# A decoder layer on one core: separate 256-wide matmuls for two of three PSUM banks, all weight sums on VectorE, another place for the first sum and another way to spread a norm row

## The chip, the cores and the metric

The kernel runs on one core of one Trainium2 chip. The metric is the device time of one launch in microseconds (us), median of several runs; each comparison runs both kernels on the same chip. The profile is one execution taken by the hardware profiler, with a time of its own.

## The reference

One decoder layer over 512 tokens of width 2048, all in float32:

```python
u = rms_norm(h, ln_mix_pre)
o_rec = hgrn2_mixer(...)               # 8 heads, gated recurrence
o_att = dilated_attention_mixer(...)   # 8 heads
h = h + rms_norm(concat(o_rec, o_att) @ w_out, ln_mix_post)
# MLP: w_up is 2048 x 11264, w_down 5632 x 2048
up = rms_norm(h, ln_ffn_pre) @ w_up
up = conv_b + sum(pad[:, j:j + S] * conv_w[j] for j in range(3))
gate, val = split(up, 2)
h = h + rms_norm((gelu(gate) * val) @ w_down, ln_ffn_post)
h = h + (p @ w_pe) * sigmoid(h @ w_pg)
```

## The kernel before

Every large product runs in fp32r (a float32 operand cut to fewer bits) with both operands split into a high and a low part: a product is hi·hi + hi·lo + lo·hi. ACT makes the high part by a cast, DVE the low part by a subtraction (`split_pair`, L623 to L628, for w_up; `split_to`, L180/L181, for activations).

**Start (L197 to L245).** The four token tiles xt of x and the row ln_mix_pre are loaded on SP's queue; the row comes four times 256 KB, a partition broadcast straight from HBM (L208). ACT squares xt, DVE scales it by the row and the inverse root (L235), PE turns it (L241) and the splits go to uT. The first weight units raw_hi are loaded in between.

**The up-projection (L619 to L960)** is the longest stage. The 512 tokens are two halves of 256 (a and b below), the 2048 inputs two halves of 1024 (eight k-blocks of 128), and the 11264 columns 44 groups j, each of two 128-column blocks (the gate's and the value's). One group is thus a 2 x 2 by 2 x 2 block product and is done with seven products instead of eight (Strassen in Winograd's form). It needs weight sums: s5 = w12 + w22, then w12 + w11, s5 + w11 (product 6) and w21 + the result (product 3). `operands(j)` makes them: before the change s5 is added on DVE for j = 1 and even j (L875), and for odd j from 3 on by a load on SP's queue and an accumulating load on POOL's queue (L870, L871); the sum of w12 is an accumulating load on POOL's queue for j > 1 (L877). w11 and w21 are summed on DVE (L880, L885). The activations' sums are made once, ahead of the stage, as eight arrays ua (`second_half`, `last_turns`), each holding the high part ah and the low part al of 256 tokens side by side.

`product(o, ops, i, first)` (L644) adds product i into a PSUM bank of 512 columns. Per k-block it issues one joined matmul of the weights' high part with [ah | al], 512 wide (L649), so that hi·al lands in the right half of the bank, and one of the low part with ah, 256 wide (L650), into the left half. Three banks serve a group: psa takes products 1, 6, 7, 4 one after another and is read after each; psb takes product 2 (read once); psc products 5 and 3. `fold` (L895) adds a psb or psc bank, 512 wide, to an SBUF copy of psa (xx, ub or uc; L897), and then the two halves of the sum together (L898). `Group` calls these in the stages begin (products 1 and 2), middle (6, 5, 7), end (4, 3) and `gate` (convolution and GELU). The stages of neighbouring groups interleave.

**Between the output projection and the stage** `second_half` finishes token tiles 2 and 3: residual (L717 to L730, with the reductions L717 and L729), scaling by ln_ffn_pre (`scale`, L735), turns on PE (`turn_half`, L703), and the activations' sums (L754 to L761). At the same time the p-embedding's products run on PE (L826 to L828) and group 0's weights are loaded (`load_group`, L639). `early_products` does products 1 and 2 of group 0 ahead; `early_sums` (L665) makes the first sums (L669 to L671), s5_0 in a tile of its own in the pool `wo`. y[t] is token tile t, 128 x 2048; its first half is `y[t][:, k1]`.

The order of the instructions on each engine is not the order of the code. A scheduler places them by priorities (`tc.high_priority`: PRI_W for weights, PRI_E for reads of PSUM) as soon as their operands and buffers are free by its own reckoning, and an engine then runs its list strictly in order: an instruction that waits holds up all behind it.

Of the kernel before, what the change touches and what calls it, by code (L numbers as in the profile page):

```python
# [10 lines left out]
F32 = mybir.dt.float32  # L11
# [4 lines left out]
ALU = mybir.AluOpType  # L16
PSUM = bass.MemoryType.PSUM

P = 128
S = 512  # L20
D = 2048
# [36 lines left out]
def trunk(ctx, tc, x, p, ln_mix_pre, w_in, lb_logits, hgrn_norm, w_out, ln_mix_post,  # L58
          ln_ffn_pre, w_up, conv_w, conv_b, w_down, ln_ffn_post, w_pe, w_pg,
          c_dist, c_level, out):  # L60
    nc = tc.nc
# [134 lines left out]

    with tc.tile_pool(name="pre", bufs=2) as pre:  # L197
        ln_b = pre.tile([P, D], F32, bufs=1, name="ln_b")
        xts = []
        for t in range(TT):  # L200
            xt = pre.tile([P, D], F32, tag="xt", bufs=4, name=f"xt{t}")
            for c in range(0, D, D if t else S):
                w = D if t else S
                nc.sync.dma_start(xt[:, c : c + w], x[0, t * P : (t + 1) * P, c : c + w])
            xts.append(xt)
            if t == 0:
                for c in range(0, D, S):
                    nc.sync.dma_start(ln_b[:, c : c + S], ln_mix_pre[0:1, c : c + S].partition_broadcast(P))  # L208
            if t < 2:
                load_unit(w_in[0], t * S, C_I, 4, S, f"hi0_{t}")  # L210
        for t in range(TT):
            xs = pre.tile([P, D], F32, tag="xs", name=f"xs{t}")
            ss = pre.tile([P, 1], F32, tag="ss", name=f"ss{t}")
            rs = pre.tile([P, 1], F32, tag="rs", name=f"rs{t}")
            if t == 0:
                s4 = pre.tile([P, 4], F32, bufs=1, name="s4")
                for g in range(4):
                    gg = slice(g * S, (g + 1) * S)
                    nc.scalar.activation(xs[:, gg], xts[t][:, gg], AF.Square, accum_out=s4[:, g : g + 1])
                nc.vector.tensor_reduce(ss, s4, axis=mybir.AxisListType.X, op=ALU.add)  # L220
            else:
                nc.scalar.activation(xs, xts[t], AF.Square, accum_out=ss)
            ahead = 1 if t else 0
            xl = [None] * 4
            for g in range(ahead):
                gg = slice(g * S, (g + 1) * S)
                xl[g] = pre.tile([P, S], F32, tag="xl", bufs=6, name=f"xl{t}_{g}")
                nc.gpsimd.tensor_tensor(xl[g], xts[t][:, gg], ln_b[:, gg], op=ALU.mult)
            power(rs, ss, 1, D)
            for g in range(4):  # L230
                gg = slice(g * S, (g + 1) * S)
                if g < ahead:
                    nc.vector.tensor_scalar(xs[:, gg], xl[g], rs[:, 0:1], None, op0=ALU.mult)
                else:
                    nc.vector.scalar_tensor_tensor(  # L235
                        xs[:, gg], xts[t][:, gg], rs[:, 0:1], ln_b[:, gg], op0=ALU.mult, op1=ALU.mult
                    )
                ps = aux.tile([P, 4, P], F32, tag="aux", name=f"xtr{t}_{g}")
                for i in range(4):
                    kb = g * 4 + i  # L240
                    nc.tensor.transpose(ps[:, i, :], xs[:, kb * P : (kb + 1) * P], ident)  # L241
                split_to(uT[g][:, :, 0, full[t]], uT[g][:, :, 1, full[t]], ps)


        hrow = pre.tile([2 * HG, P], F32, bufs=1, name="hrow")  # L245
        nc.sync.dma_start(hrow[0:HG, :], lb_logits.rearrange("a (h k) -> (a h) k", k=P))
        nc.sync.dma_start(hrow[HG : 2 * HG, :], hgrn_norm.rearrange("a (h k) -> (a h) k", k=P))
        hps = aux.tile([P, S], F32, tag="aux", name="hps")
        nc.tensor.transpose(hps[:, : 2 * HG], hrow, ident[: 2 * HG, : 2 * HG])
        nc.vector.tensor_copy(norm_c, hps[:, HG : 2 * HG])  # L250
        lg = pre.tile([P, HG], F32, bufs=1, name="lg")
        nc.vector.tensor_copy(lg, hps[:, :HG])
        dl = pre.tile([P, HG], F32, bufs=1, name="dl")
        nc.vector.tensor_tensor(dl, lg, lg, op=ALU.subtract)
        nc.scalar.activation(dl, dl, AF.Exp)
        inv = pre.tile([P, HG], F32, bufs=1, name="inv")
        nc.vector.reciprocal(inv, dl)
        nc.vector.tensor_tensor(dl, dl, inv, op=ALU.mult)
        nc.vector.tensor_tensor(lb_c, dl, dl, op=ALU.subtract)
        nc.vector.tensor_scalar(oml_c, lb_c, -1.0, 1.0, op0=ALU.mult, op1=ALU.add)  # L260
        crow = pre.tile([2 * NFB, 4, P], F32, bufs=1, name="crow")
        for j in range(3):
            nc.sync.dma_start(crow[:, j, :], conv_w[0, j, :].rearrange("(c k) -> c k", k=P))
        nc.sync.dma_start(crow[:, 3, :], conv_b[0, :].rearrange("(c k) -> c k", k=P))
        cps = aux.tile([P, 4, 2 * NFB], F32, tag="aux", name="cps")
        for j in range(4):
            nc.tensor.transpose(cps[:, j, :], crow[:, j, :], ident[: 2 * NFB, : 2 * NFB])
        nc.vector.tensor_copy(conv_c, cps)
# [352 lines left out]
    H8 = KB // 2  # L621
# [8 lines left out]
    def weights(j, k, i):  # L630
        c = i * DFF + j * P
        return w_up[0, k * H8 * P : (k + 1) * H8 * P, c : c + P].rearrange("(k p) n -> p k n", p=P)
# [8 lines left out]
        return raws  # L641


    def product(o, ops, i, first):  # L644
        hi, lo = ops[i]
        for kb in range(H8):
            u = ua[i][kb // 4][:, kb % 4] if i == 4 else ua[i][:, kb]
            both = u.rearrange("p a t -> p (a t)")
            nc.tensor.matmul(o, hi[:, kb, :], both, start=first and kb == 0, stop=False, skip_group_check=True)  # L649
            nc.tensor.matmul(  # L650
                o[:, : 2 * P], lo[:, kb, :], u[:, 0, :], start=False, stop=kb == H8 - 1, skip_group_check=True
            )

    def early_products():
        raws, ops = load_group(0, rawp), {}
# [6 lines left out]
        product(b, ops, 2, True)  # L662
        return raws, ops, a, b

    def early_sums(first, pool):  # L665
        raws, ops = first[:2]
        s5 = pool.tile([P, H8, P], F32, tag="s5e", bufs=1, name="s5_0")
        w11, w12, w22 = raws[0][:, :, 0, :], raws[0][:, :, 1, :], raws[1][:, :, 1, :]
        nc.vector.tensor_tensor(s5, w12, w22, op=ALU.add)  # L669
        nc.vector.tensor_tensor(w12, w11, w12, op=ALU.add)  # L670
        nc.vector.tensor_tensor(w11, s5, w11, op=ALU.add)  # L671
        ops[6] = split_pair(w11, P, "u0_6")
        ops[5] = split_pair(s5, P, "u0_5")
# [5 lines left out]
    with tc.tile_pool(name="wo", bufs=2) as wo:  # L679
# [158 lines left out]
        first = early_products()  # L838
        last_turns(2)
        for _ in late:  # L840
            pass
        early_sums(first, wo)
        last_turns(3)

    homes = {"A": act_slot, "B": lambda tag, name: b_slot(int(tag[1:]), name)}
# [12 lines left out]
    with tc.tile_pool(name="ml", bufs=2) as ml:  # L858
        HT = 2 * P

        def operands(j):
            r1, r2 = first[0] if j == 0 else load_group(j, ml if j % 2 else rawp)
            w11, w12, w21, w22 = r1[:, :, 0, :], r1[:, :, 1, :], r2[:, :, 0, :], r2[:, :, 1, :]
            ops = first[1] if j == 0 else {}
            with tc.high_priority(PRI_W):
                if j:
                    by_dma = (j > 1 and j % 2 == 1, j > 1)
                    s5 = ml.tile([P, H8, P], F32, tag="s5", name=f"s5_{j}")
                    if by_dma[0]:
                        nc.sync.dma_start(s5, weights(j, 0, 1))  # L870
                        nc.gpsimd.dma_start(s5, weights(j, 1, 1), accum_op=ALU.add)  # L871
                    ops[1] = split_pair(w11, P, f"u{j}_1")
                    ops[2] = split_pair(w21, P, f"u{j}_2")
                    if not by_dma[0]:
                        nc.vector.tensor_tensor(s5, w12, w22, op=ALU.add)  # L875
                    if by_dma[1]:
                        nc.gpsimd.dma_start(w12, weights(j, 0, 0), accum_op=ALU.add)  # L877
                    else:
                        nc.vector.tensor_tensor(w12, w11, w12, op=ALU.add)
                    nc.vector.tensor_tensor(w11, s5, w11, op=ALU.add)  # L880
                    ops[6] = split_pair(w11, P, f"u{j}_6")
                    ops[5] = split_pair(s5, P, f"u{j}_5")
                ops[7] = split_pair(w12, P, f"u{j}_7")
                ops[4] = split_pair(w22, P, f"u{j}_4")
                nc.vector.tensor_tensor(w21, w21, w11, op=ALU.add)  # L885
                ops[3] = split_pair(w21, P, f"u{j}_3")
            return ops
# [6 lines left out]

        def fold(dst, src, ps):  # L895
            with tc.high_priority(PRI_E):
                nc.vector.tensor_tensor(src, src, ps, op=ALU.add)  # L897
                nc.vector.tensor_tensor(dst, src[:, :HT], src[:, HT:], op=ALU.add)  # L898

        class Group:  # L900
# [207 lines left out]
```

## Time and profile before

| what | value |
|---|---|
| median of 3 runs | 2534.76 us (2534.52 to 2535.32) |
| profiled execution, its own time | 2539.58 us |
| span of that execution, first to last instruction | 2537.8 us |
| mean granted TensorE clock | 0.993 of full speed |
| instructions | 31312 |
| busy: PE, PEld (weight loads), DVE, ACT, POOL | 98 %, 82 %, 63 %, 44 %, 9 % |
| HBM traffic | 335 MB read, 28 MB written |

A busy share is an average over stages: in the up-projection DVE is far busier than over the whole span. Matmuls are pipelined, so the record of one lasts longer than the distance from its start to the next one's; what a stream of them costs is read from the starts. What stands behind an arrow in brackets is the time an engine was idle ahead of a row and what ended it.

### The profile page before, as it was taken

How to read it: one execution, taken by the hardware profiler on the slowest of the kernel's cores; microseconds unless marked ns; L12 is line 12 of the kernel's file. 1: busy time of each engine (PE TensorE's matmuls, PEld its weight loads, DVE VectorE, ACT ScalarE, POOL GpSimd, SP SyncE). 2: the span in 40 equal slices, each digit the busy share in tenths (PEclk: the TensorE clock that was granted, in tenths of full speed). 3: DMA queues.
4: the chain of work that ended last, by engine and by line, in shares of the span. 5: the costliest groups of instructions: out<-in, count | busy, mean ns of one | idle time of the engine just before them, and what ended most of it. 6: DMA issues, size and time to landing. Idle time of an engine off the chain costs nothing. (4 is left out here: it accounts for less than half of the span.)

```text
span 2537.8 us, 31312 instructions
## 1 busy us (share of the span) xinstructions
PE 2477.9 (98%) x12357; PEld 2087.4 (82%) x12357; DVE 1590.5 (63%) x2199; ACT 1122.9 (44%) x1538; POOL 233.3 (9%) x255
## 2 busy tenths in 40 slices
PE   8999999999999977999999999999999999999999
PEld 6888888888888866888888888888888888887787
DVE  5467377434352567898998988989852233347733
ACT  4454365233342454655555555555542232124421
POOL 1000000000000010111111111111110000002300
PEclk9999999999999998999999999999999999999999
DMA  5222222322234574887877878778654233245642
GB/s 197 89 84 92 91 84 92 112 92 83 92 116 154 201 235 121 182 186 167 179 170 170 183 162 179 173 170 185 158 196 140 100 125 125 99 141 195 210 134 88
DMA packets 397280, 364.86 MB, mean 144 GB/s; under 512 B 9948, under 2 KB 318156, under 8 KB 396492
## 3 DMA queue, kind: packets, MB, share of 16 engines
q1 hardware_dynamic: 316412, 286.82, 36.3%
q0 software_dynamic: 75568, 67.12, 14.2%
q10 hardware_dynamic: 5152, 8.92, 1.0%
q8 instruction: 97, 1.59, 0.2%
q14 instruction: 51, 0.42, 0.1%
HBM read 335.03 MB, written 27.79 MB: 143 GB/s over the span
## 5 line engine op out<-in xcount | busy, mean ns | idle before, releaser
L649 PE MATMUL psa<-ua,hi_u 128*128 128x512 f32 x1408 | 504.1, 399 | 3.6 <-ACT ub L892 1.7
L626 ACT CAST hi_u<-raw_u 128x1024 fp32r<-128x1024 f32 x264 | 277.7, 1052 | 304.2 <-PE psa L649 161.2
L650 PE MATMUL psa<-ua,lo_u 128*128 128x256 f32 x1408 | 395.7, 281 | 1.3 <-DVE lo_u L627 1.3
L627 DVE TENSOR_TENSOR lo_u<-raw_u,hi_u 128x1024 fp32r<-128x1024 f32 x264 | 322.2, 1221 | 43.8 <-ACT hi_u L626 43.3
L649 PEld LDWEIGHTS psa<-ua,hi_u 128*128 128x128 f32 x1408 | 264.5, 188 | 70.2 <-ACT ub L892 2.4
L650 PEld LDWEIGHTS psa<-ua,lo_u 128*128 128x128 f32 x1408 | 266.0, 189 | 2.0 <-DVE lo_u L627 2.0
L649 PE MATMUL psc<-ua,hi_u 128*128 128x512 f32 x704 | 252.7, 399 | 0.0
L135 DVE TENSOR_TENSOR lo_dn<-raw_dn,hi_dn 128x1024 fp32r<-128x1024 f32 x72 | 88.1, 1224 | 230.7 <-ACT hi_dn L134 230.6
L168 PE MATMUL ps_dn<-lo_dn,gT 128*128 128x512 f32 x576 | 224.2, 389 | 0.6 <-DVE lo_dn L135 0.6
L169 PE MATMUL ps_dn<-hi_dn,gT 128*128 128x512 f32 x576 | 224.1, 389 | 0.0
L167 PE MATMUL ps_dn<-hi_dn,gT 128*128 128x512 f32 x576 | 223.9, 389 | 0.0
L650 PE MATMUL psc<-ua,lo_u 128*128 128x256 f32 x704 | 197.7, 281 | 0.0
L134 ACT CAST hi_dn<-raw_dn 128x1024 fp32r<-128x1024 f32 x72 | 75.8, 1054 | 242.6 <-PE ps_dn L169 234.2
L649 PEld LDWEIGHTS psc<-ua,hi_u 128*128 128x128 f32 x704 | 132.3, 188 | 32.9
L650 PEld LDWEIGHTS psc<-ua,lo_u 128*128 128x128 f32 x704 | 133.0, 189 | 0.1
L168 PEld LDWEIGHTS ps_dn<-lo_dn,gT 128*128 128x128 f32 x576 | 108.1, 188 | 23.6 <-DVE lo_dn L135 1.0
L167 PEld LDWEIGHTS ps_dn<-hi_dn,gT 128*128 128x128 f32 x576 | 108.0, 188 | 22.4
L649 PE MATMUL psb<-ua,hi_u 128*128 128x512 f32 x352 | 126.5, 399 | 0.0
L169 PEld LDWEIGHTS ps_dn<-hi_dn,gT 128*128 128x128 f32 x576 | 108.1, 188 | 22.3
L135 DVE TENSOR_TENSOR lo_wo<-raw_wo,hi_wo 128x1024 fp32r<-128x1024 f32 x48 | 58.7, 1224 | 76.3 <-ACT hi_wo L134 76.3
L135 DVE TENSOR_TENSOR lo_pg<-raw_pg,hi_pg 128x1024 fp32r<-128x1024 f32 x40 | 51.6, 1290 | 85.9 <-ACT hi_pg L134 85.9
L167 PE MATMUL ps_pg<-hi_pg,h2T 128*128 128x512 f32 x256 | 100.2, 391 | 3.3 <-ACT h2T L180 3.3
(328 smaller groups left out, 5412.0 us busy)
## 6 DMA issues: line engine op xcount, KB each, us to landing
raw_u<-in_w_up SPq DMA_DIRECT2D x176, 512.0 KB, 5.4
raw_dn<-in_w_down SPq DMA_DIRECT2D x36, 1024.0 KB, 5.0
raw_wo<-in_w_out SPq DMA_DIRECT2D x24, 1024.0 KB, 5.1
raw_u<-in_w_up POOLq DMA_DIRECT2D x42, 512.0 KB, 6.3
raw_pg<-in_w_pg SPq DMA_DIRECT2D x20, 1024.0 KB, 5.0
raw_dl<-in_w_down SPq DMA_DIRECT2D x16, 1024.0 KB, 5.1
g_dram<-cv POOLq DMA_DIRECT2D x44, 256.0 KB, 5.3
gs<-g_dram POOLq DMA_DIRECT2D x22, 512.0 KB, 5.1
```

Of the source, the lines that this page charges most:

```text
L134: nc.scalar.copy(hi, raw[:, k0 : k0 + step, :])
L135: nc.vector.tensor_tensor(lo, raw[:, k0 : k0 + step, :], hi.bitcast(F32), op=ALU.subtract)
L167: nc.tensor.matmul(ps[t], ah[:, cols], hi[:, i, :], start=kb == 0, stop=False)
L168: nc.tensor.matmul(ps[t], ah[:, cols], lo[:, i, :], start=False, stop=False)
L169: nc.tensor.matmul(ps[t], al[:, cols], hi[:, i, :], start=False, stop=kb == nkb - 1)
L626: nc.scalar.copy(hi, src)
L627: nc.vector.tensor_tensor(lo, src, hi.bitcast(F32), op=ALU.subtract)
L649: nc.tensor.matmul(o, hi[:, kb, :], both, start=first and kb == 0, stop=False, skip_group_check=True)
L650: nc.tensor.matmul(o[:, : 2 * P], lo[:, kb, :], u[:, 0, :], start=False, stop=kb == H8 - 1, skip_group_check=True)
```

## The change

Four edits:

1. `product` joins only for products 1, 6, 7 and 4 (bank psa). For products 2, 5 and 3 (psb, psc) hi·al is a separate matmul, 256 wide, into the left half too; per k-block three 256-wide matmuls stand for one of 512 and one of 256. `fold` then adds 256 columns of the bank instead of 512.
2. `operands` makes s5 and the sum of w12 on DVE for every j from 1 on; the loads of L870, L871 and L877 go.
3. `early_sums` puts s5_0 into the first half of y[0], whose last reader there is the turn and the sums of token tile 2; its own tile goes.
4. The row ln_mix_pre is loaded once, 8 KB on ACT's queue, and spread over the partitions by four matmuls with a row of ones (one 512-column PSUM bank each) and four DVE copies.

The sums of edit 2 for j = 1 were on DVE already. The diff:

```diff
+        ln_row = pre.tile([1, D], F32, bufs=1, name="ln_row")
+        nc.scalar.dma_start(ln_row, ln_mix_pre[0:1, :])
+        one_row = pre.tile([1, P], F32, bufs=1, name="one_row")
+        nc.gpsimd.memset(one_row, 1.0)
+        for c in range(0, D, S):
+            ps = aux.tile([P, S], F32, tag="aux", name=f"lnb{c}")
+            nc.tensor.matmul(ps, one_row, ln_row[:, c : c + S], start=True, stop=True)
+            nc.vector.tensor_copy(ln_b[:, c : c + S], ps)
...
-            if t == 0:
-                for c in range(0, D, S):
-                    nc.sync.dma_start(ln_b[:, c : c + S], ln_mix_pre[0:1, c : c + S].partition_broadcast(P))
...
+    JOINED = (1, 6, 7, 4)
     def product(o, ops, i, first):
...
-            both = u.rearrange("p a t -> p (a t)")
-            nc.tensor.matmul(o, hi[:, kb, :], both, start=first and kb == 0, stop=False, skip_group_check=True)
-            nc.tensor.matmul(
-                o[:, : 2 * P], lo[:, kb, :], u[:, 0, :], start=False, stop=kb == H8 - 1, skip_group_check=True
-            )
+            ah, al, h = u[:, 0, :], u[:, 1, :], o[:, : 2 * P]
+            if i in JOINED:
+                both = u.rearrange("p a t -> p (a t)")
+                nc.tensor.matmul(o, hi[:, kb, :], both, start=first and kb == 0, stop=False, skip_group_check=True)
+            else:
+                nc.tensor.matmul(h, hi[:, kb, :], ah, start=first and kb == 0, stop=False, skip_group_check=True)
+                nc.tensor.matmul(h, hi[:, kb, :], al, start=False, stop=False, skip_group_check=True)
+            nc.tensor.matmul(h, lo[:, kb, :], ah, start=False, stop=kb == H8 - 1, skip_group_check=True)
...
-    def early_sums(first, pool):
+    def early_sums(first, s5):
         raws, ops = first[:2]
-        s5 = pool.tile([P, H8, P], F32, tag="s5e", bufs=1, name="s5_0")
...
-        early_sums(first, wo)
+        early_sums(first, y[0][:, k1].rearrange("p (a b) -> p a b", b=P))
...
-                    by_dma = (j > 1 and j % 2 == 1, j > 1)
                     s5 = ml.tile([P, H8, P], F32, tag="s5", name=f"s5_{j}")
-                    if by_dma[0]:
-                        nc.sync.dma_start(s5, weights(j, 0, 1))
-                        nc.gpsimd.dma_start(s5, weights(j, 1, 1), accum_op=ALU.add)
...
-                    if not by_dma[0]:
-                        nc.vector.tensor_tensor(s5, w12, w22, op=ALU.add)
-                    if by_dma[1]:
-                        nc.gpsimd.dma_start(w12, weights(j, 0, 0), accum_op=ALU.add)
-                    else:
-                        nc.vector.tensor_tensor(w12, w11, w12, op=ALU.add)
+                    nc.vector.tensor_tensor(s5, w12, w22, op=ALU.add)
+                    nc.vector.tensor_tensor(w12, w11, w12, op=ALU.add)
...
-                nc.vector.tensor_tensor(src, src, ps, op=ALU.add)
+                nc.vector.tensor_tensor(src[:, :HT], src[:, :HT], ps[:, :HT], op=ALU.add)
```

The edits move instructions on DVE at three places. Lines of the changed kernel are 5 higher in `split_pair` (L627 is L632), 10 higher in `residual` and `scale` (L721 is L731, L735 is L745), and 2 higher in `fold` (L897 is L899).

**Before the stage**, DVE's order where token tile 2 (y_5814, in the changed kernel y_5826) and tile 3 (y_5815, y_5827) get their residual and scaling; s_0 is s5_0, raw_u_0 and raw_u_1 are group 0's weights. Before:

```order
L721 SCALAR_TENSOR_TENSOR y_5815<-y_5815,st_5823,xp_1_6830 128x512
L627 TENSOR_TENSOR lo_u_1_7103<-raw_u_0_7094,hi_u_1_7102 128x1024
L721 SCALAR_TENSOR_TENSOR y_5815<-y_5815,st_5823,xp_2_6836 128x512
L669 TENSOR_TENSOR s_0_7220<-raw_u_0_7094,raw_u_1_7097 128x1024
L670 TENSOR_TENSOR raw_u_0_7094<-raw_u_0_7094 128x8x128
L671 TENSOR_TENSOR raw_u_0_7094<-s_0_7220,raw_u_0_7094 128x8x128
L627 TENSOR_TENSOR lo_u_2_7107<-raw_u_1_7097,hi_u_2_7106 128x1024
L721 SCALAR_TENSOR_TENSOR y_5815<-y_5815,st_5823,xp_3_6842 128x512
L885 TENSOR_TENSOR raw_u_1_7097<-raw_u_1_7097,raw_u_0_7094 128x8x128
L729 TENSOR_REDUCE st_5822<-sq_5818 128x1
L735 SCALAR_TENSOR_TENSOR y_5814<-y_5814,st_5822,lnf_b 128x512 x4
```

Now, the same stretch:

```order
L731 SCALAR_TENSOR_TENSOR y_5827<-y_5827,st_5835,xp_1_6842 128x512
L632 TENSOR_TENSOR lo_u_1_7115<-raw_u_0_7106,hi_u_1_7114 128x1024
L731 SCALAR_TENSOR_TENSOR y_5827<-y_5827,st_5835,xp_2_6848 128x512
L632 TENSOR_TENSOR lo_u_2_7119<-raw_u_1_7109,hi_u_2_7118 128x1024
L731 SCALAR_TENSOR_TENSOR y_5827<-y_5827,st_5835,xp_3_6854 128x512
L739 TENSOR_REDUCE st_5834<-sq_5830 128x1
L745 SCALAR_TENSOR_TENSOR y_5826<-y_5826,st_5834,lnf_b 128x512 x4
```

and 8 rows further on, where the first sum now stands (y_5824 is y[0]):

```order
L771 SCALAR_TENSOR_TENSOR y_5824<-y_5826,y_5824 128x1024
L181 TENSOR_TENSOR ua_6837<-u6t_6986,ua_6837 128x4x128
L181 TENSOR_TENSOR ua_6837<-u6t_6993,ua_6837 128x4x128
L739 TENSOR_REDUCE st_5835<-sq_5831 128x1
L679 TENSOR_TENSOR y_5824<-raw_u_0_7106,raw_u_1_7109 128x1024
L745 SCALAR_TENSOR_TENSOR y_5827<-y_5827,st_5835,lnf_b 128x512 x3
```

The first three sums and w21's (L669 to L671, L885; now L679 to L681, L887) left the place ahead of tile 2's reduction and scaling and stand behind tile 2's turns, among the steps of tile 3.

**At the start**, DVE's first rows (xs and xt are token tile 0, uT its splits, lo_hi the first weights' low parts). Before:

```order
L220 TENSOR_REDUCE ss_118<-s_120 128x1
L235 SCALAR_TENSOR_TENSOR xs_117<-xt_98,rs_119,ln_b 128x512 x4
L181 TENSOR_TENSOR uT_80<-xtr_0_129,uT_80 128x4x128
L181 TENSOR_TENSOR uT_81<-xtr_1_137,uT_81 128x4x128
L181 TENSOR_TENSOR uT_82<-xtr_2_145,uT_82 128x4x128
L135 TENSOR_TENSOR lo_hi_0_0_321<-raw_hi_0_107,hi_hi_0_0_320 128x1024
L135 TENSOR_TENSOR lo_hi_0_2_349<-raw_hi_0_107,hi_hi_0_2_348 128x1024
```

Now:

```order
L225 TENSOR_REDUCE ss_130<-s_132 128x1
L206 COPY ln_b<-lnb_102 128x512
L240 SCALAR_TENSOR_TENSOR xs_129<-xt_114,rs_131,ln_b 128x512
L135 TENSOR_TENSOR lo_hi_0_0_333<-raw_hi_0_119,hi_hi_0_0_332 128x1024
L135 TENSOR_TENSOR lo_hi_0_2_361<-raw_hi_0_119,hi_hi_0_2_360 128x1024
L206 COPY ln_b<-lnb_105 128x512
L206 COPY ln_b<-lnb_108 128x512
L206 COPY ln_b<-lnb_111 128x512
L240 SCALAR_TENSOR_TENSOR xs_129<-xt_114,rs_131,ln_b 128x512
```

Four copies came in, and two low parts that wait for the first weight unit moved ahead of three of the four pieces of xs.

**In the stage**, one group on DVE (group 9 with its neighbours; s_9 and s_10 are the sums s5). Before:

```order
L627 TENSOR_TENSOR lo_u_2_8752<-raw_u_1_8741,hi_u_2_8751 128x1024
L875 TENSOR_TENSOR s_10_8926<-raw_u_0_8920,raw_u_1_8923 128x1024
L885 TENSOR_TENSOR raw_u_1_8741<-raw_u_1_8741,raw_u_0_8738 128x8x128
L627 TENSOR_TENSOR lo_u_6_8758<-raw_u_0_8738,hi_u_6_8757 128x1024
L897 TENSOR_TENSOR uc_8833<-uc_8833,psc_8782 128x512
L897 TENSOR_TENSOR xx_8853<-xx_8853,psb_8781 128x512
```

Now:

```order
L632 TENSOR_TENSOR lo_u_2_8958<-raw_u_1_8949,hi_u_2_8957 128x1024
L880 TENSOR_TENSOR s_10_9157<-raw_u_0_9151,raw_u_1_9154 128x1024
L887 TENSOR_TENSOR raw_u_1_8949<-raw_u_1_8949,raw_u_0_8946 128x8x128
L632 TENSOR_TENSOR lo_u_6_8965<-raw_u_0_8946,hi_u_6_8964 128x1024
L881 TENSOR_TENSOR raw_u_0_9151<-raw_u_0_9151 128x8x128
L632 TENSOR_TENSOR lo_u_5_8969<-s_9_8952,hi_u_5_8968 128x1024
L899 TENSOR_TENSOR uc_9048<-uc_9048,psc_8989 128x256
L899 TENSOR_TENSOR xx_9068<-xx_9068,psb_8988 128x256
```

The sum of w12 (L881) is a DVE row of every group now, and the folds read 256 columns.

## Rows read from the trace of the kernel before

**Rows 1.** The page's first part: busy us, share of the span, instructions.

```profile
PE 2477.9 (98%) x12357; PEld 2087.4 (82%) x12357; DVE 1590.5 (63%) x2199; ACT 1122.9 (44%) x1538; POOL 233.3 (9%) x255
```

**Rows 2.** Stretches (length; busy PE, PEld, DVE, ACT, POOL; clock, DMA, GB/s): stage, group.

```profile
1010.00:1858.00 848.00, 847.19 (x4792) 733.84 (x4791) 764.12 (x923) 484.86 (x604) 125.88 (x109) 1.00 0.78 172
...
1238.84:1258.62 19.78, 19.78 (x114) 17.16 (x113) 18.36 (x23) 11.23 (x14) 3.18 (x2) 1.00 0.88 181
```

**Rows 3.** Timeline of PE (start, length), a product 2: pairs in a row.

```profile
1301.97 0.40 PE L649 MATMUL psb<-ua,hi_u 128*128 128x512 f32 x1
...
1303.03 0.40 PE L649 MATMUL psb<-ua,hi_u 128*128 128x512 f32 x1
```

**Rows 4.** Timeline of PE in the attention's scores: first, last and next after six.

```profile
533.64 0.28 PE L525 MATMUL a_s<-ak,aq 128*128 128x256 f32 x1
...
534.23 0.28 PE L527 MATMUL a_s<-ak,aq 128*128 128x256 f32 x1
534.35 0.27 PE L546 MATMUL a_t<-ident,a_sm 128*128 128x128 f32 x1
```

**Rows 5.** Timeline of PE in the attention's output.

```profile
562.02 0.53 PE L564 MATMUL a_o<-a_pT,av 128*128 128x256 f32 x3
...
562.39 0.44 PE L564 MATMUL a_o<-a_pT,av 128*128 128x128 f32 x3
```

**Rows 6.** Groups by line and shape on DVE (busy, mean ns, idle before), 1010 to 1858.

```profile
L627 DVE TENSOR_TENSOR lo_u<-raw_u,hi_u 128x1024 fp32r<-128x1024 f32 x255 | 311.3, 1221 | 40.3 <-ACT hi_u L626 39.8
...
L897 DVE TENSOR_TENSOR ub<-ub,psc 128x512 f32<-128x512 f32 x43 | 29.6, 687 | 11.6 <-PE psc L650 11.6
...
L897 DVE TENSOR_TENSOR xx<-xx,psb 128x512 f32<-128x512 f32 x42 | 28.7, 684 | 6.6 <-PE psb L650 6.6
...
L898 DVE TENSOR_TENSOR cu<-ub 128x256 f32<-128x256 f32 x43 | 18.3, 425 | 1.4
```

**Rows 7.** Timeline of DVE, 934 to 954 us (idle before in brackets).

```profile
945.29 1.22 DVE L669 TENSOR_TENSOR s<-raw_u,raw_u 128x1024 f32<-128x1024 f32 x1 [9.36 <-DMA raw_u<-in_w_up]
...
951.88 0.15 DVE L729 TENSOR_REDUCE st<-sq 128x1 f32<-128x4 f32 x1
953.00 1.42 DVE L735 SCALAR_TENSOR_TENSOR y<-y,st,lnf_b 128x512 f32<-128x512 f32 x2 [0.96 <-POOL st L83]
```

**Rows 8.** Timeline of PE at its longest wait, and the stretch 948 to 956.

```profile
953.89 1.09 PE L703 MATMUL u3t<-ident,y 128*128 128x128 f32 x4 [12.70 <-DVE y L735]
954.63 0.78 PE L828 MATMUL pe<-hi_pe,pT 128*128 128x512 f32 x1
...
948.00:956.00 8.00, 2.10 (x10) 1.95 (x10) 7.04 (x10) 0.59 (x1) 1.86 (x4) 0.50 0.18 66
```

**Rows 9.** Timeline of ACT: the end of tile 2's last square.

```profile
941.79 0.19 ACT L728 ACTIVATION_READ_ACCUMULATOR jh<-y 128x1 f32 x1
```

**Rows 10.** Stretches and timelines of SP and DVE, 953 us up to group 1.

```profile
953.00:988.20 35.20, 23.88 (x128) 20.25 (x128) 31.45 (x40) 18.59 (x34) 3.44 (x7) 0.76 0.27 90
...
977.87 0.99 SPq L639 DMA_DIRECT2D raw_u<-in_w_up  x2
...
987.48 4.75 SPq L639 DMA_DIRECT2D raw_u<-in_w_up  x4
...
990.00:1000.00 10.00, 6.48 (x34) 4.89 (x32) 3.31 (x3) 3.06 (x4) 0.00 (x0) 1.00 1.09 280
...
997.92 1.22 DVE L875 TENSOR_TENSOR s<-raw_u,raw_u 128x1024 f32<-128x1024 f32 x1 [4.41 <-DMA raw_u<-in_w_up]
```

**Rows 11.** Start of the kernel: three stretches, and DVE's first scaling.

```profile
4.00:6.00 2.00, 0.00 (x0) 0.00 (x0) 0.00 (x0) 1.30 (x5) 0.00 (x0) 1.00 0.82 243
...
8.83 0.75 DVE L235 SCALAR_TENSOR_TENSOR xs<-xt,rs,ln_b 128x512 f32<-128x512 f32 x1 [1.69 <-DMA ln_b<-in_ln_mix_pre]
...
10.00:12.00 2.00, 2.00 (x11) 1.75 (x10) 2.00 (x4) 0.83 (x2) 0.00 (x0) 1.00 1.08 419
...
20.00:34.00 14.00, 13.67 (x75) 10.65 (x75) 14.00 (x21) 9.82 (x14) 6.89 (x6) 0.97 0.64 226
```

## The prediction

> **What bounds the kernel now.** I read the page's busy shares first: PE is busy 98 % of the span, DVE 63 % [rows 1]. Then busy time by stretch: from 1010 to 1858 us, 43 of the 44 column groups, PE has 847.19 of 848.00 us at granted clock 1.00, DVE 764.12 (90 %), ACT 57 % [rows 2]. One group takes 19.78 us; DVE works 18.36 us of it in an even group, where it makes the sum s5 itself [rows 2]. Here only PE's own work counts, as long as DVE keeps up. Last the timelines of the two places where PE stands still and where the change moves something: the start, and the stretch from 940 to 1004 us, in which the second half of the normalised tokens is prepared for the first group.
>
> What I work out stands against the profiled execution's 2539.58 us (span 2537.80 and 1.78 around it), 4.8 above the median of 2534.76; I carry the difference over to the median. A measurement of this kernel can tell about 0.2 % (5 us) from no change.
>
> **The products 2, 5 and 3.** Eight k-blocks each lose one 512-wide matmul and gain two 256-wide ones: 3 x 8 x 44 = 1056 pairs become triples. A pair now takes, start to start, (1303.03 − 1301.97)/3 = 353 ns [rows 3]. Triples with the same operands (hi·hi, hi·lo, lo·hi into one place, 256 wide) exist in the attention: the scores start 120 ns apart, six matmuls in 0.71 us, 360 for three at the steady pitch, 355 over the whole [rows 4]. Three 256-wide matmuls of the attention's output take 562.39 − 562.02 = 370 [rows 5]. So a triple costs +2 to +17 ns more; I take +6.7, the steady pitch of the scores, whose order of operands is this one. 1056 x 6.7 = **+7.0 us**, bounds +1.5 and +17.6. A third weight load goes with it. PEld is busy 733.84 us with 4791 loads, 153 ns each [rows 2], yet the scores, with a load for each matmul, start every 120 ns [rows 4]: part of a load's record lies beside the one before, and I price the third at nothing beyond the pitch. If the records did stand in line, a triple would take 459 ns, and 1056 of them +112 us more, which rows 4 exclude. The Trainium skill ("TensorE: Matmul & The Clock Gate", LDWEIGHTS (loading the stationary operand)) speaks against more loads: it says a load takes about columns/1.2 ns, some 107 ns for these 128 whatever the matmul's width. By it alone three loads are about 320 ns, just under the 360 of the row, and the sum stays as it is.
>
> **The weight sums and folds on DVE.** Per group DVE takes over the w12 sum, and for odd groups s5: 1.5 sums of 1.22 us (L669's length [rows 7]) on average, +1.83. The three folds shrink from 512 wide (0.68) to 256 (0.42): 3 x 0.26 = −0.79 [rows 6]. DVE's mean of 764.12/848 x 19.78 = 17.82 becomes 18.86 us, in a period of 19.78 + 24 x 0.0067 = 19.94: 95 %. Its present idle time (84 us) is to almost a half waits for ACT's casts (39.8 us [rows 6]), which run ahead of PE and wait for free buffers; that is slack and can shrink. Only the folds' waits for PE (11.6 + 6.6 us, 0.42 per group) are forced, and 18.86 + 0.42 = 19.28 still fits. I cost it at **0**; PE's stream is the cover, and what it costs without that cover is rival C. The 63 accumulating loads of POOL's queue (512 KB) and 21 of SP go; nothing on PE waits for them now, as PE has no gap in this stage [rows 2], so this too is 0.
>
> **The first sums' place.** This is the main gain. Group 0's sum s5 (L669) stands in DVE's order before the last residual piece, the reduction L729 and the scaling L735 of token tile 2. DVE comes to it at 936 us and waits 9.36 us for group 0's last load; then come the four sums and one lo split, and L735 starts at 953.00 [rows 7]. PE waits 12.70 us for it, from 941.2 to 953.9 [rows 8], and then turns at half clock: the granted clock is 0.50 from 948 to 956 [rows 8] of full speed, the lower of its two levels. ACT had the last square of tile 2 ready at 941.98 [rows 9]. With the sum in y[0] it must wait until tile 2's turns have read that half: in the changed order it stands 12 rows behind L735, where it stood 7 ahead. So the reduction can start at 942, the power on POOL ends some 0.9 us later (951.88 to 953.00 is 1.12 now), and L735 starts at about 943.2, 9.8 us earlier.
>
> Not all of it arrives. The sums (4 x 1.22 = 4.9 us) now lie between tile 3's steps, in a DVE chain with only 35.20 − 31.45 = 3.75 us idle from 953 to 988 [rows 10]: 1 to 5 us come back, and product 6 of group 0, which ends this chain at 988, comes near 980. Then the next limit: group 1's four loads wait for tile 3's last turn and leave SP from 987.48 on; the fourth half lands with L875's start at 997.92, after 4.41 us of waiting [rows 10]. The loads start earlier as the turn does (about 980), but at 280 GB/s they share the way with group 2's, which leave SP at 977.87 already [rows 10]: 6 halves, 3.15 MB, take 11 us, so the last lands at 990 to 991. I take **−7 us**. Bounds: −10 if the whole 9.8 us arrive, −3 if the sums' 4.9 us come back in full and 2 us on the loads.
>
> **The norm row.** Four 256 KB loads (1 MB, L208) leave SP's queue; the loads behind them come earlier by what 1.05 MB take: at 243 to 419 GB/s 4.3 to 2.5 us, and the faster rate is that of the stretch where those loads run [rows 11]. The first scaling waits 1.69 us for the row now and starts at 8.83 [rows 11]. New on the path are four f32 matmuls of one row and four DVE copies ahead of xs. The trace has no such matmul; the nearest are the f32 turns, four of 128 columns in 1.09 us at half clock [rows 8], so four of 512 columns take some 4 us. PE has nothing to do before that first scaling, and ACT squares x's first pieces from 4 to 6 us [rows 11]; if the 8 KB row lands with them there is room, so I price the matmuls at nothing (without that room, 4 us). A copy takes at most the 0.69 us of a 512-wide fold [rows 6], four 2.7. And ACT now squares xt1 ahead of the casts of uT, and DVE has no gap from 20 to 34 us [rows 11], so the copies eat most of what the earlier loads give. I take **−0.5**, between −2.5 (the whole 1 MB at the faster rate) and +2.7 (all copies on the path, nothing saved).
>
> **Sum:** +7.0 − 7 − 0.5 = −0.5 us: 2539.1 in the profiled execution, **2534.3** by the median: no change that can be told.
>
> **Rivals.** B: the triple costs what the attention's output shows, +17.6 us, and the sum is +10: **2545**, slower. For it: three different streams into one half of a bank, as there. Against it: the scores, whose stream is closest in kind.
>
> C, also slower: DVE becomes the bound. Mechanism: the casts' waits (39.8 us, 0.93 per group) are needed after all, because a lo split can't be done before its cast, and a cast not before PE frees a buffer. Then 18.86 + 0.42 + 0.93 = 20.21 us against 19.94: +0.27 x 43 = +12, **2546**. It decides once DVE's forced idle time is above 1.08 us per group. For it: 95 % busy. Against it: in even groups DVE had 18.36 of 19.78 with no PE gap.
>
> D: only columns count, the split is free. A 256-wide matmul is half of a 512-wide one and the pair's 353 becomes the 355 that the six scores show as a whole: +1.5 us, sum −6, **2528.8**, faster. The Trainium skill ("TensorE: Matmul & The Clock Gate", Back-to-back issue gap) has such a rule: a gap of about N/2.4 + 2.5 ns at the full clock. An estimate by that page is +2.5 ns per triple, 2.6 us in all. Against it: the steady pitch of 120.
>
> E: both gains come at their far ends (−10 and −2.5) with +7: −5.5, **2529.3**, just faster.
>
> F: the transition gains nothing, since group 1's loads land as late as now: +6.5, **2541**, slower. Against it: they wait on a turn that itself moves.
>
> **Numbers.** Forecast 0.38, B 0.16, C 0.11, D 0.24, E 0.06, F 0.05. Faster D and E 0.30, same 0.38, slower B, C and F 0.32. The range goes from 2525 (D with 4 us of the other terms' far ends) to 2548 (C and B with 2 us on top). The likeliest case's own range is 2530 to 2539.
>
> **What would show it.** In the changed profile: starts in products 2, 5, 3 are 120 ns apart and a group takes 19.94 us; psa's pairs stay at 353 ns. DVE is at about 95 % and PE at 99.9 % in the groups; a PE gap there released by a lo split or a fold means C. The 12.70 us wait for u3t shrinks to about 3, and the last of group 1's loads lands about 7 us earlier. The first projection's matmuls from 45 us on stand within 2 us of where they do now. A triple at 370 or 355 settles B or D. I am wrong if the transition keeps its length or a group takes over 20.2 us.

## The result: 1.1 % slower, outside the predicted range

The changed kernel takes 2563.06 us (median of 4 runs, 2559.96 to 2565.92), the kernel before beside it 2535.04. The ratio is 1.0109, 95 % interval 1.0095 to 1.0124. The profiled execution has a span of 2564.1 us against 2537.8: +26.3 us. Where they arise, from the starts of the same instructions in both traces (the third stretch, from the first matmul behind group 2's product 2 to psa's last, holds some 42 groups):

| stretch | before, us | after, us | difference |
|---|---|---|---|
| start to the output projection's last matmul | 922.68 | 922.74 | +0.1 |
| from there to the first matmul behind group 2's product 2 | 104.40 | 98.33 | −6.1 |
| 42 groups, to psa's last matmul | 831.07 | 862.98 | +31.9 |
| from there to the end | 679.66 | 680.07 | +0.4 |

The other stretches came within a few us of the forecast. The 42 groups by stretch (after; columns as in [rows 2]):

```profile
1021.07:1884.05 862.98, 847.98 (x5696) 774.53 (x5695) 784.53 (x967) 472.19 (x590) 25.69 (x46) 1.00 0.41 116
```

PE is idle for 15 us here, where [rows 2] had less than 1; an engine's record also covers the tail of its last matmul, so by starts the gaps are longer. DVE is busy for 91 % only, not the 95 % that I had worked out: it waits, and PE waits for it. The page's costliest groups of the changed kernel hold two of PE's, psa's and psc's first matmuls (busy, mean ns, idle before and what ended it):

```profile
L659 PE MATMUL psa<-ua,hi_u 128*128 128x512 f32 x1408 | 505.7, 400 | 3.2 <-ACT ub L894 1.5
...
L661 PE MATMUL psc<-ua,hi_u 128*128 128x256 f32 x704 | 204.2, 290 | 14.8 <-DVE uc L899 13.5
```

Before, psc's first matmul had none:

```profile
L649 PE MATMUL psc<-ua,hi_u 128*128 128x512 f32 x704 | 252.7, 399 | 0.0
```

The new idle time stands ahead of psc's first matmul, and the fold uc (L899) ends it. psc takes product 5, the fold uc reads it, and product 3 goes on in the same bank: product 3 must wait for that read. The longest such gap, on PE and on DVE:

```profile
1187.44 0.28 PE L663 MATMUL psa<-ua,lo_u 128*128 128x256 f32 x1
1189.54 0.38 PE L661 MATMUL psc<-ua,hi_u 128*128 128x256 f32 x1 [1.83 <-DVE uc L899]
```

```profile
1183.39 1.23 DVE L880 TENSOR_TENSOR s<-raw_u,raw_u 128x1024 f32<-128x1024 f32 x1 [1.97 <-DMA raw_u<-in_w_up]
1184.54 1.22 DVE L887 TENSOR_TENSOR raw_u<-raw_u,raw_u 128x1024 f32<-128x1024 f32 x1
1185.67 1.22 DVE L632 TENSOR_TENSOR lo_u<-raw_u,hi_u 128x1024 fp32r<-128x1024 f32 x1
1186.81 1.22 DVE L881 TENSOR_TENSOR raw_u<-raw_u 128x1024 f32<-128x1024 f32 x1
1187.94 1.22 DVE L632 TENSOR_TENSOR lo_u<-s,hi_u 128x1024 fp32r<-128x1024 f32 x1
1189.08 0.42 DVE L899 TENSOR_TENSOR uc<-uc,psc 128x256 f32<-128x256 f32 x1
...
1191.54 0.42 DVE L935 TENSOR_TENSOR cu<-cu,psa 128x256 f32<-128x256 f32 x1
1194.21 0.42 DVE L899 TENSOR_TENSOR ub<-ub,psc 128x256 f32<-128x256 f32 x1 [2.26 <-PE psc L663]
```

Read it downwards. DVE stands 1.97 us at s5 of the next group, which waits for a load; behind it in the list come four more pieces of weight work, among them the new w12 sum (L881), and only then uc, although ACT had finished uc's copy of psa at 1180.65 and product 5 was done before that. PE started its last matmul of product 4 at 1187.44 and has nothing left. Then the roles turn: PE does product 3, and DVE, which has only five pieces (2.5 us) before the next fold ub, waits for product 3, here 2.26 us, 0.76 on average. The two waits feed each other in a round: DVE is late with uc, PE late with product 3, DVE late with ub and all that follows, the next uc among it. The gap stands ahead of psc in nearly all of the 42 groups, mostly 0.4 to 0.6 us from start to start, where 0.12 is usual (period 20.2 to 20.5 us), and up to 2.1 where a load is late; beyond the usual distance they add up to 21 us. At the longest gap, and at no other, the clock falls too: the granted clock is 1.00 from 1186 to 1189 and 0.50, the lower of its two levels, from 1190.7 to 1194.0, where product 3's matmuls start 0.21 us apart and not 0.12. That is part of DVE's 2.26 us there and costs, as an estimate from these starts, some 1.5 us. DVE's waits over the 42 groups:

```profile
L632 DVE TENSOR_TENSOR lo_u<-raw_u,hi_u 128x1024 fp32r<-128x1024 f32 x250 | 305.5, 1222 | 16.7 <-ACT hi_u L631 13.0
...
L880 DVE TENSOR_TENSOR s<-raw_u,raw_u 128x1024 f32<-128x1024 f32 x40 | 49.0, 1225 | 20.3 <-DMA raw_u<-in_w_up 20.3
...
L899 DVE TENSOR_TENSOR ub<-ub,psc 128x256 f32<-128x256 f32 x42 | 17.7, 421 | 32.1 <-PE psc L663 32.1
```

Per group that is 784.53/42 = 18.68 us of work, 0.76 waiting for product 3, 0.48 for loads, 0.31 for casts and as much in short gaps: 20.5, above PE's 19.93, which is the group's period in every variant below with separate matmuls whose PE has no gap. The waits for PE at the folds were 11.6 + 6.6 us before [rows 6].

The stretch ahead of the groups went as the prediction's steps had it. L745 is L735 [rows 7], L713 turns as L703 did [rows 8]:

```profile
942.22 0.75 DVE L745 SCALAR_TENSOR_TENSOR y<-y,st,lnf_b 128x512 f32<-128x512 f32 x1 [1.18 <-DMA h_dram<-y]
944.22 2.08 DVE L745 SCALAR_TENSOR_TENSOR y<-y,st,lnf_b 128x512 f32<-128x512 f32 x3 [1.24 <-DMA h_dram<-y]
...
955.40 1.22 DVE L679 TENSOR_TENSOR y<-raw_u,raw_u 128x1024 f32<-128x1024 f32 x1
...
990.75 1.23 DVE L880 TENSOR_TENSOR s<-raw_u,raw_u 128x1024 f32<-128x1024 f32 x1 [2.16 <-DMA raw_u<-in_w_up]
```

```profile
943.12 0.63 PE L713 MATMUL u3t<-ident,y 128*128 128x128 f32 x4 [1.86 <-DVE y L745]
```

The scaling starts at 942.22 (forecast 943.2, before 953.00) and group 1's last load lands at 990.75 (forecast 990 to 991, before 997.92). The start of the kernel, by contrast, is about 3 us late:

```profile
7.82 0.68 DVE L206 COPY ln_b<-lnb 128x512 f32<-128x512 f32 x1
...
13.04 2.36 DVE L135 TENSOR_TENSOR lo_hi<-raw_hi,hi_hi 128x1024 fp32r<-128x1024 f32 x2 [3.42 <-ACT hi_hi L134]
15.31 1.88 DVE L206 COPY ln_b<-lnb 128x512 f32<-128x512 f32 x3
17.11 0.75 DVE L240 SCALAR_TENSOR_TENSOR xs<-xt,rs,ln_b 128x512 f32<-128x512 f32 x1
```

```profile
3.32 7.16 PE L205 MATMUL lnb<-ln_row,one_row 1*128 1x512 f32 x8 [3.32 <-DMA ln_row<-in_ln_mix_pre]
```

The three copies wait 3.42 us behind low parts whose weights have not come, and xs with them. At the output projection's end the 3 us are gone, but the row is not shown to have done that. They go between the output projection's first matmul (726.06 before, 728.88 now) and its 200th (785.78 and 785.58). The profile of before has there a wait of 1.0 us (L525) and a granted clock of 0.50 from 734.2 to 737.5, and the new one has neither. The profiles of edit 1 alone and edit 2 alone below, with the old row, have no such fall of the clock there either.

### The profile page after: what moved, and what is told of

It is laid out like the page before. It is cut to its first block, busy times and chain, and to the rows that moved or that the text cites. A ratio compares the mean times of both kernels' runs of the same rounds, so it can differ in the third digit from the quotient of the medians.

```text
span 2564.1 us, 33289 instructions
## 1 busy us (share of the span) xinstructions
PE 2504.4 (98%) x13421; PEld 2151.2 (84%) x13421; DVE 1628.7 (64%) x2266; ACT 1120.7 (44%) x1538; POOL 133.7 (5%) x193
## 5 line engine op out<-in xcount | busy, mean ns | idle before, releaser
L632 DVE TENSOR_TENSOR lo_u<-raw_u,hi_u 128x1024 fp32r<-128x1024 f32 x264 | 322.6, 1222 | 21.8 <-ACT hi_u L631 17.9
L661 PE MATMUL psc<-ua,hi_u 128*128 128x256 f32 x704 | 204.2, 290 | 14.8 <-DVE uc L899 13.5
L662 PE MATMUL psc<-ua,hi_u 128*128 128x256 f32 x704 | 200.1, 284 | 0.0
L661 PEld LDWEIGHTS psc<-ua,hi_u 128*128 128x128 f32 x704 | 135.1, 192 | 29.9 <-DVE uc L899 27.5
L662 PEld LDWEIGHTS psc<-ua,hi_u 128*128 128x128 f32 x704 | 135.4, 192 | 0.1
```

Source lines behind the costliest of these rows:

```text
L632: nc.vector.tensor_tensor(lo, src, hi.bitcast(F32), op=ALU.subtract)
L661: nc.tensor.matmul(h, hi[:, kb, :], ah, start=first and kb == 0, stop=False, skip_group_check=True)
L662: nc.tensor.matmul(h, hi[:, kb, :], al, start=False, stop=False, skip_group_check=True)
```

## The experiments

Theory H, in its first form: the next group's sums stand ahead of the fold uc, and product 3 waits for that fold. Rivals: T, DVE's work as such is too much for the period; M, the separate matmuls and their weight loads cost more than their pitch. All ratios are to the kernel before on the same chip.

**Edit 1 alone**: `product` and `fold` as in the change, all else as before.

> The kernel before with only the separate matmuls and the 256-wide folds (edit 1). Theory H (the changed kernel loses its time to the order on VectorE: the next group's sums stand ahead of the fold that frees bank psc, and product 3 waits for that fold): VectorE has less work here than before (17.0 us of a 19.95 us group), so no wait appears and the time is before + 1056 x 6.7 ns = 2542 us, groups of 19.95 us. Rival T (VectorE's total work is too much for the period, in whatever order): the same 2542. Rival M (the third matmul and its weight load cost more than their pitch): before + 32 = 2567 us.

Measured 2543.8 us, ratio 1.0034 (1.0020 to 1.0048), and groups of 19.93 us without a gap. M falls: 19.93 − 19.785 is 0.145 us for 24 triples, 6.0 ns each. In the changed kernel itself the triples start 120 ns apart.

**Edit 2 alone**: the sums of `operands` as in the change.

> The kernel before with only all weight sums on VectorE (edit 2). VectorE's work per group becomes 17.82 + 1.83 = 19.65 us of 19.79. H: the sums stand ahead of the fold of psc as in the changed kernel, whose VectorE was idle 1.87 us per group for such dependences; with the same idle time a group takes 21.5 us, +1.7 x 43: 2608 us, with PE gaps ahead of product 3. T: only the work and the folds' waits of 0.42 us count, 20.07 us per group, +0.28 x 43: 2547 us, and the gaps are spread over all products. M: no matmul is added, so 2535 us.

Measured 2539.5 us, ratio 1.0028 (1.0008 to 1.0047). My 2608 for H was far off, and T's 2547 is above it too. DVE is busy 805.30 of 834.83 us here (96 %), more than in the changed kernel, and PE has gaps of 3 us in all, 2.4 of them ahead of product 3:

```profile
L649 PE MATMUL psc<-ua,hi_u 128*128 128x512 f32 x674 | 241.6, 398 | 2.6 <-DVE uc L889 2.4
```

The trace of this kernel's DVE shows why they are so small, between the same two folds:

```profile
1182.26 1.22 DVE L627 TENSOR_TENSOR lo_u<-s,hi_u 128x1024 fp32r<-128x1024 f32 x1
1183.40 0.68 DVE L889 TENSOR_TENSOR uc<-uc,psc 128x512 f32<-128x512 f32 x1
...
1186.73 0.69 DVE L941 SCALAR_TENSOR_TENSOR cv<-cv,cv 128x512 f32<-128x512 f32 x1
1187.33 0.69 DVE L889 TENSOR_TENSOR ub<-ub,psc 128x512 f32<-128x512 f32 x1
```

The sums stand ahead of uc as there, but from uc to ub DVE has 3.93 us of work, more than product 3 takes (8 x 353 ns = 2.8 us), so ub waits 0.3 us in sum over the 42 groups where it was 32.1. H got its second form from this run: the loss needs both, uc late behind the sums, and DVE idle between uc and ub. The time alone flatters this kernel: its joined pairs start 351 ns apart on average and not 353 (the last section), some 6 us in all, and its gaps ahead of product 3 are 5.4 us from start to start, against 21.

**Edit 2 undone** in the changed kernel.

> The changed kernel with the accumulating loads back in place of the sums (edit 2 undone). H and T: the 21 us of PE gaps ahead of product 3 and what the clock loses behind them go; before - 6.4 (the stretch before the groups) + 7 (matmuls) = 2535.5 us. M: the gaps' time stays with the matmuls, 2560 us or more.

Measured 2540.8 us, ratio 1.0026 (1.0010 to 1.0041), groups of 19.93 us, PE busy 836.09 of 836.27. The median lies 5 us above H's number and 19 below M's. The gaps belong to the sums: PE's idle time ahead of product 3 is 0 here and with edit 1 alone, 2.4 us with edit 2 alone and 13.5 with all edits.

**The fold put first**: the work is the changed kernel's to the instruction, only the order of the list differs. The line raises all three folds, uc, ub and xx.

```diff
         def fold(dst, src, ps):
-            with tc.high_priority(PRI_E):
+            with tc.high_priority(4500):
```

> The changed kernel with one number changed: the folds get a higher priority (4500) than the weight work (4000). On VectorE the fold uc, which frees psc, then stands ahead of the next group's two sums and of two low parts; the work is the same to the instruction. H: the gaps ahead of product 3 go, a group takes 19.95 to 20.05 us: 2538 to 2542 us. T: the work of VectorE is unchanged, so the time stays at 2560 to 2566 us and the gaps move to other products.

Measured 2538.7 us, ratio 1.0017 (1.0001 to 1.0032): 24 us of the change's 28 are gone, and every group takes 19.93 us. T falls with it: DVE does 787.54 us of work in 836.23 (94 %) and PE has no gap.

```profile
1022.50:1858.73 836.23, 836.11 (x5696) 773.35 (x5695) 787.54 (x965) 472.04 (x590) 25.69 (x46) 1.00 0.42 120
```

```profile
1197.37 1.23 DVE L632 TENSOR_TENSOR lo_u<-raw_u,hi_u 128x1024 fp32r<-128x1024 f32 x1 [0.32 <-ACT hi_u L631]
1198.51 0.41 DVE L899 TENSOR_TENSOR uc<-uc,psc 128x256 f32<-128x256 f32 x1
1198.84 1.22 DVE L887 TENSOR_TENSOR raw_u<-raw_u,raw_u 128x1024 f32<-128x1024 f32 x1
...
1201.45 1.22 DVE L880 TENSOR_TENSOR s<-raw_u,raw_u 128x1024 f32<-128x1024 f32 x1
```

uc now stands ahead of the sums, which no longer wait for their load, and 9 us of DVE's list lie between uc and ub.

**A bank of its own for product 3**: DVE's order stays, but product 3 has nothing to wait for.

```diff
-                product(self.c, self.ops, 3, False)
-                fold(self.cu[0][:, HT:], self.u2, self.c)
+                d = aux.tile([P, S], F32, tag="aux", name=f"psd_{self.j}")
+                product(d, self.ops, 3, True)
+                fold(self.cu[0][:, HT:], self.u2, d)
```

and in `middle` psc's left half is added to u2 under PRI_E, ahead of `self.u2 = u2`.

> The changed kernel with a PSUM bank of its own for product 3 (psd): psc's left half is added to ub early, psd at the end, one more 256-wide VectorE addition per group (0.33 us). VectorE's order keeps the next group's sums ahead of the fold uc. H: PE no longer waits for that fold, the gaps ahead of product 3 go, groups of 19.93 to 20.0 us, 2538 to 2541 us. T (VectorE's work is the bound whatever waits): VectorE has more work, so 2563 + 0.33 x 43 = 2577 us at most, 2560 at least.

Measured 2545.7 us, ratio 1.0043 (1.0022 to 1.0065): above H's 2541 and below T's 2560. Once more, for its profile:

> The kernel with a bank of its own for product 3 once more, for a profile that can be compared: its times were 2545.7 us, 17 under the changed kernel and 7 over the fold put first. H: no gap ahead of product 3 that a fold uc ends; what is left stands ahead of other products.

2538.8 us in this one execution, and all but two of the groups within 0.02 us of 19.93. No fold ends a gap any more, although DVE has more to do than in the changed kernel (793.39 us) and s5 waits for its load as long as there:

```profile
L659 PE MATMUL psa<-ua,hi_u 128*128 128x512 f32 x1330 | 475.4, 398 | 0.7 <-ACT uc L894 0.7
...
L661 PE MATMUL psd<-ua,hi_u 128*128 128x256 f32 x333 | 94.2, 283 | 0.0
```

```profile
L880 DVE TENSOR_TENSOR s<-raw_u,raw_u 128x1024 f32<-128x1024 f32 x40 | 49.0, 1226 | 23.0 <-DMA raw_u<-in_w_up 22.9
...
L899 DVE TENSOR_TENSOR ub<-ub,psd 128x256 f32<-128x256 f32 x42 | 17.4, 415 | 0.1
```

So it is the shared bank that couples the two waits. Why the timed runs lie 7 us above this execution is open.

**Half of edit 2**: w12 by an accumulating load for j > 1, s5 on DVE throughout.

> The changed kernel with the sum of w12 back as an accumulating load for j > 1, s5 on VectorE in every group (half of edit 2). VectorE's loop from one fold uc to the next loses 1.14 us. In the changed kernel that loop is 18.68 us of work + 0.76 waiting for product 3 + 0.48 for loads + 0.4 for casts = 20.3 us; less 1.14 it is 19.2, under the 19.93 of PE. H: no gaps, 2538 to 2541 us. Rival (position alone counts: s5, which waits for a load, still stands ahead of the fold): gaps of 0.3 us or more per group stay, 2550 us or more.

Measured 2538.2 us, ratio 1.0020 (1.0001 to 1.0038), groups of 19.93 us. s5 waits for its load 22.2 us in all, as in the changed kernel, and costs nothing: one piece of 1.14 us less in the round is enough.

**Edit 1 undone** in the changed kernel; it tests the second form of H.

> The changed kernel with the joined matmuls and 512-wide folds back in all products (edit 1 undone; sums, place and row stay). VectorE's work per group is 19.65 us, 0.8 more than in the changed kernel, and the sums stand ahead of the fold uc as there. But between the folds uc and ub stand 3.9 us of other VectorE work (2.9 us in the changed kernel), more than the 2.8 us of product 3. Loop theory (H in its present form: VectorE idles between uc and ub while product 3 runs, and that idle time, with the waits for loads and casts, lifts its round above PE's): no such idle time, groups of 19.85 us as with the sums alone; before + 4 - 6 = 2533 us. Rival (the position of the sums ahead of uc is enough): gaps ahead of product 3 as in the changed kernel, 2550 us or more.

Measured 2535.6 us, ratio 1.0018 (1.0001 to 1.0035). ub waits 0.4 us for product 3 in sum over 42 groups, and 3.0 us of idle time ahead of product 3 are left:

```profile
L655 PE MATMUL psc<-ua,hi_u 128*128 128x512 f32 x704 | 252.8, 399 | 3.1 <-DVE uc L894 3.0
```

The sums ahead of uc are not enough by themselves for the changed kernel's 13.5 us. Here too the joined pairs start 350 to 351 ns apart, so the time flatters this kernel by some 6 us; the idle time ahead of product 3 shows it without that.

**The loads of w22 ahead of w21**, for k = 1 and j > 0:

```diff
-            for i in range(2):
+            for i in (0, 1) if j == 0 or k == 0 else (1, 0):
```

> The changed kernel with the second K half's loads of groups 1 to 43 in the other order (w22 before w21). In VectorE's order s5 then stands ahead of the low part lo_2 and one low part (lo_5) moves behind uc. Loop theory: the wait of s5 for its load (20.3 us in 42 groups) goes, and 0.5 us less per round brings VectorE's round to 19.9, about PE's 19.93: 2538 to 2543 us. Rival (two sums ahead of uc are enough): 2555 us or more.

Measured 2567.3 us, ratio 1.0132 (1.0111 to 1.0154): a miss for both. The order followed the loads: s5 moved up ahead of lo_2, met its load as late as ever (17.9 us in all), and now lo_2 was behind it. Product 3's gaps went, product 2's came:

```profile
L663 PE MATMUL psb<-ua,lo_u 128*128 128x256 f32 x328 | 96.9, 295 | 19.1 <-DVE lo_u L632 19.0
```

**The place alone** (edit 3).

> The kernel before with only the first sum's place in y[0] (edit 3). H: PE's wait for the first turns of tile 2 shrinks and the first group's product comes 6 to 7 us earlier, as in the changed kernel; the groups stay at 19.79 us and nothing takes it back: before - 6.5 us, 0.9974 of it. Rival: the gain of the stretch belongs to the sums or the row and the place alone gives less than 2 us: 0.999 or more.

Measured 2529.5 us, ratio 0.9975 (0.9955 to 0.9995): −5.6 us, and in the trace 98.3 us instead of 104.4 from the output projection's last matmul to the first matmul behind group 2's product 2. This edit alone gives the gain that the changed kernel shows there.

**The row alone** (edit 4), and **place and row together** (edits 3 and 4).

> The kernel before with only the norm row spread by matmuls (edit 4). Prediction's term: -0.5 us. By the changed kernel's trace the first projection's matmuls come 1 to 3 us later, so the new reading is +1 to +3 us, 1.0004 to 1.0012, unless a later wait takes it up. Too near to the spread of the runs for the time alone; the place of the first projection's 200th matmul in the trace tells (216.00 us before).

> The kernel before with edits 3 and 4 (place and row), the candidate: before - 5.5 for the place and between -3 and +3 for the row: 0.997 to 0.999 of before.

Measured 2527.6 us, 0.9981 (0.9959 to 1.0003), and 2530.5 us, 0.9986 (0.9967 to 1.0004). The first projection's matmul that starts at 216.00 us before starts at 216.67 and 217.21 us, so the row costs some 1 us there, and the 3 us of the changed kernel are its far end. The times of both are not told from no change, and groups of two paces, of which the last section tells, spread them. The place alone is the one version whose interval lies below the kernel before.

## Why the prediction was wrong

- **Products 2, 5 and 3, +7.0: right.** The triples start every 120 ns, +6 ns each; rivals B and D are out (370 and 355 were not seen). The lower bound was a little off: 355 ns for a triple give +1.8 us, not +1.5, which changes no choice.
- **The first sum's place, −7: right**, −6.1 in the trace and −5.6 by itself, through the very rows I had named: the scaling 10.8 us earlier, then group 1's loads as the next limit.
- **The norm row, −0.5: wrong, with little weight.** The matmuls took 7.16 us, eight instructions of 0.9 us at granted clock 1.00, and not 4, and three of the copies stand behind low parts: +3 us at the first projection's 200th matmul. That nothing of it is left at the end of the output projection is luck as far as the runs show: the profile of before lost as much there to a wait and a fall of the clock.
- **The weight sums on DVE at 0: this is the step that failed.** I compared DVE's work with the period (18.86 + 0.42 against 19.94) and took PE's stream as the cover for whatever order DVE works in. The work came out right (18.68 us), and it fits: with the fold put first DVE is busy for 94 % and PE has no gap. But an engine works its list strictly in order, and I had the list: in the changed order, the sums L880 and L881 stand ahead of the fold uc in every group, where before only the s5 of even groups did. I did not ask who waits for uc. Product 3 does, in the same bank, and ub then waits for product 3. That round costs 27 us (862.98 against 836.23 with the fold put first), of which I had none. The signs named ahead did show it: a PE gap released by a fold, which I had put down to C, and groups of over 20.2 us.
- **Rival C had the side and not the mechanism.** It gave 0.11 and +12 us to waits for casts. The casts' waits fell from 39.8 us [rows 6] to 13.0, as slack does. Its threshold of 1.08 us of forced idle time per group was useful: DVE's idle time came out at (862.98 − 784.53)/42 = 1.87.

## What to carry to other kernels

A busy share below the period says that the work fits, not that the order does. When work moves to an engine that runs its list in order, look in the new list for what now stands ahead of an instruction that frees a PSUM bank or a buffer, and follow who waits for it: two reads of one bank, with a product of another engine between them, make a round, and its length (work plus the waits inside it) has to stay under the period. A small edit cures such a round (the read's priority, a second bank, or one piece of work less); each was worth 17 to 25 us here.

## What the runs showed of the hardware that was not expected

The joined pairs run at two paces in the same program. In the kernel with the row alone the profiled execution has groups of 19.41 us throughout, pairs 346 ns apart, where [rows 3] show 353:

```profile
1301.44 0.39 PE L654 MATMUL psa<-ua,hi_u 128*128 128x512 f32 x1
1301.67 0.28 PE L655 MATMUL psa<-ua,lo_u 128*128 128x256 f32 x1
...
1302.48 0.39 PE L654 MATMUL psc<-ua,hi_u 128*128 128x512 f32 x1
```

With place and row it changes from one to the other on the way, at the same granted clock of 1.00, with no gap:

```profile
1120.00:1139.78 19.78, 19.78 (x114) 17.14 (x113) 18.66 (x25) 11.24 (x14) 3.73 (x3) 1.00 1.16 221
1300.00:1319.41 19.41, 19.41 (x115) 17.11 (x114) 18.12 (x22) 11.25 (x14) 2.20 (x2) 1.00 0.67 151
```

0.37 us in 43 groups are 16 us, about the distance from the lowest times of the kernel before (2518 us, on the chips of the experiments) to its usual 2535. No kernel with separate matmuls went below 2535 us in its timed runs, and in all of their profiles psa's pairs start 353 ns apart on average. But the two kernels with joined matmuls and all sums on DVE (edit 2 alone, edit 1 undone) did not go below 2533 us in twenty timed runs either, with pairs of 350 to 351 ns on average. So the runs don't show which edit gives the faster pace up, nor what sets it, and no experiment was made on it. One more reading: in the changed kernel's groups the granted clock fell once, behind the longest PE gap (2.1 us from start to start), and not behind the others, which reach 1.7 us; whether the length decides is not shown.
